# A hybrid SSD, attention and FFN layer on one core: the passage into the FFN and the end of the kernel in written-out orders, and sums, splits and norm weights moved

## The chip, the cores and the metric

The kernel runs on one core of a Trainium2 chip. The metric is the device time of one execution in microseconds, as the median of several runs. Times of single instructions come from one profiled execution of the kernel before; its rows are quoted as the profile prints them, with microseconds from the start of the span. PE is the matrix engine (TensorE), PEld its weight loads, DVE the VectorE, ACT the ScalarE, POOL the GpSimd, SP the engine that issues most DMAs.

## The reference

One layer on a sequence of 1024 tokens of 1024 features, batch 1, all float32:

```python
h = rmsnorm(x, norm_mix_w) * (1 + sc_m) + sh_m
z, xbc, dt_raw, q, k, v = split(h @ w_in)
x = x + g_m * (concat([ssd_mixer(z, xbc, dt_raw), chunk_attention(q, k, v)]) @ w_out)
h = rmsnorm(x, norm_ffn_w) * (1 + sc_f) + sh_f
u = causal_dwconv(h @ w_up, conv_w)          # width 3, FFN 2 x 2816
g, val = split(u)
x = x + g_f * ((silu(g) * val) @ w_down)
out = rmsnorm(x, final_norm_w)
```

The scales, shifts and gates (`sc_m`, `g_f` and so on) come from a product of `silu(c)` with `w_ada`. The change concerns one place in `ssd_mixer` (the cumulative sums of dt), the start of `h @ w_up`, the product with `w_down`, the last residual and the last norm.

## The kernel before

**Products.** Every large product is made in three passes: each operand is split into a high part (ACT copies it into the matrix engine's reduced float32 type) and a low part (DVE subtracts the high part from the operand), and `mm3` (lines 75 to 78) issues high x high, high x low and low x high. So before a product can start, ACT and DVE each have an instruction to do per operand tile, and these are the names that the profile shows: `w` for split weights (hi by ACT, lo by DVE), `tH`/`tL` for split activations.

**The FFN.** `h @ w_up` and the product with `w_down` are done by a Strassen-like scheme with seven products of half the size in each direction, called P1, P2, P3, Q4, Q5, Q6, Q7 (`PRODS`, line 1113). In the up part a *unit* (class `Unit`) is 128 columns of `w_up`; units go in pairs u0 and u1, one for the gate half and one for the value half, in 11 pairs. `sums` forms the weight sums of a unit (rows 4 to 7 of its buffer `b`: `ya` for u0, `xs` for u1), `prep` splits two weight blocks into one *home*, `product` issues the 12 matmuls of a product into a PSUM bank (`uX`, `uY` or `uZ`), and `post` takes the bank off (`cv`, `cg`). Split weights live in a ring of five homes (`HOMES`, `FIRST`, `AGAIN`, lines 1087 to 1095); a new split waits until the product that last used its home is done. The activations that the products need (`t2`, `t3`, `t4`, `b22`) are sums of normalised rows, and for the last rows they are made and split (`h_last`) while the first pair is already on the PE. The raw `t2` lies in the buffer that `cg` takes over.

**Down part.** Seven products (lines 1526 to 1548) with four PSUM banks each (`dn`), the contraction in six steps `m` (11 blocks of 128, so the last step has one block). `split_pair` loads and splits both operands of a step. Results pile up in p1, u2, u3 and q5, four tiles of 128 rows x 512 columns each; `gate` multiplies such a tile by the gate row and adds x (read back from DRAM as `x1d` into two buffers `xts`, on the SP queue); `final` squares a finished row of tiles (ACT), makes the factor (DVE adds two means, POOL raises to -1/2), scales both halves by factor and norm weight (DVE) and stores them (SP).

**What sets the order.** A planner places the instructions of each engine by its own cost model, except between `V.on = A.on = T.on = True` and `False`: there DVE, ACT and PE issue in the order in which the Python code is written (class `InOrder`, from line 45; such instructions carry line 58 in the profile). In the kernel before such a stretch begins at line 800 with the z part and the dt sums (to line 997 on PE, to line 1026 on DVE and ACT), and another is the passage into the FFN, on PE from line 1228, on DVE and ACT from line 1236, to line 1293. From there to the end the planner is free.

Of the kernel before, what the change touches and what calls it, by code (L numbers as in the profile page):

```python
# [16 lines left out]
P = 128  # L17
# [47 lines left out]
def tile_block(ctx: ExitStack, tc: tile.TileContext, x, crep, pk, w_ada, w_first, w_ft, w_z,  # L65
# [1022 lines left out]
    FIRST, AGAIN = (0, 1, 2, 0, 1, 3, 4), (2, 0, 1, 3, 4)  # L1088
# [27 lines left out]
    class Unit:  # L1116
# [29 lines left out]
        def post(self, p, ps):  # L1146
# [11 lines left out]
            elif p == "Q7":  # L1158
                V.tensor_tensor(self.v[:, 512:S], ps, self.v[:, 0:512], ALU.subtract)
                V.tensor_tensor(self.v[:, 512:S], self.v[:, 512:S], self.ps["Z"], ALU.subtract)  # L1160
# [7 lines left out]
            self.done.add(p)  # L1168

# [91 lines left out]
    def h_last(n, src):  # L1261
        for j in range(2):
            h_split(n, src, slice(2 * j, 2 * j + 2))

    h_last("t2", "t2")
    u0.product("P2")
    u1.prep("Q5", "Q6")
# [4 lines left out]
    for u in units:  # L1272
        u.product("Q5")
    h_last("t3", "b12")
    for u in units:
        u.sums((6,))
    for u in units:
        u.prep("Q7", "Q4")
    for u in units:
        u.product("Q6")  # L1280
    h_last("t4", "b21")
    for u in units:
        u.sums((7,))

# [6 lines left out]
    h_last("b22", "b22")  # L1291
    prep_s4(units)
    V.on = A.on = T.on = False
# [77 lines left out]
    for q in range(KH):  # L1371
        if q > 0:
            units = [Unit(q), Unit(KH + q)]
            for u in units:
                u.sums()
        order = ("Q7", "Q4", "P3") if q == 0 else ("P1", "Q6", "Q5", "Q7", "P2", "Q4", "P3")
# [57 lines left out]
    def split_pair(p, m):  # L1434
        ab = [wsplit(t, kn(m)) for t in operands(p, m)]
# [10 lines left out]
    def product(p, ps, ready=(), tail=False, between=None):  # L1446
        last = []
        for m in RM:
# [3 lines left out]
            for k in range(2 * m, 2 * m + kn(m)):  # L1452
                if tail and m >= NM - 2:
                    last.append((ab, k))
                else:
                    step(ps, ab, k, R4)
        return last
# [12 lines left out]
    def final(st, lo, hi):  # L1470
        t = fins[st % 3]
        m = [stat(), stat()]
        for dh, src in enumerate((lo, hi)):
            A.activation(t[:, halves[dh]], src, AF.Square, scale=1.0 / 32.0, accum_out=m[dh])
        r = rstd2(m)
        for dh, src in enumerate((lo, hi)):
            V.scalar_tensor_tensor(t[:, halves[dh]], src, r, fnr[:, halves[dh]], op0=ALU.mult,
                                   op1=ALU.mult)
            nc.sync.dma_start(out[st * P:(st + 1) * P, halves[dh]], t[:, halves[dh]])
# [56 lines left out]
    product("P3", Z)  # L1536
    W = banks("d")
    last = product("P2", W, tail=True)
    for st in R4:
        V.tensor_tensor(u2[st], u2[st], Z[st], ALU.add)  # L1540
    for st in R4:
        gate(u2[st], 4 + st, 0)
        final(4 + st, u2[st], q5[st])
    for st in R4:
        for ab, k in last:
            step(W, ab, k, (st,))
        e = xt_()
        V.tensor_tensor(e, W[st], gf[:, halves[0]], ALU.mult)
        V.tensor_tensor(p1[st], p1[st], e, ALU.add)
        final(st, p1[st], u3[st])  # L1550
# [54 lines left out]
```

## Time and profile before

| what | value |
|---|---|
| median of 3 runs | 1210.14 us (1209.7 to 1210.21) |
| the profiled execution's own time | 1210.66 us |
| its span, first to last instruction | 1208.9 us |
| mean granted clock of the PE | 0.993 |
| PE busy | 1159.7 us (96% of the span) |
| DVE busy | 941.8 us (78%) |
| ACT busy | 594.7 us (49%) |
| POOL busy | 195.3 us (16%) |

A timeline row gives the start, the time taken, the engine, the line, the operation with out<-in, the shapes and the count; at its end in brackets the idle time of the engine just before it and what ended that time. Consecutive matmuls overlap: one of 512 columns takes 0.39 us from start to end, and the next starts 0.227 us after it. A row of the windows view gives, for each engine, the busy time in a stretch and the number of instructions, then the granted clock of the PE and the DMA engines' share.

### The profile page before, as it was taken

The page shows a single profiled execution, that of the slowest core. Times are in us where ns is not written, and L with a number is a line of the kernel's source. Part 1 is how long each engine was busy: PE and PEld are TensorE (multiplying, and loading weights), DVE is VectorE, ACT ScalarE, POOL GpSimd, SP SyncE. Part 2 cuts the span into 40 slices and gives each one's busy share as a digit, 9 for nine tenths or more (in the row PEclk, how much of TensorE's full clock was granted, in tenths as well). Part 3 has the DMA queues.
Part 4 walks back from the last instruction along what each step waited for, and adds up shares of the span by engine and source line. Part 5 has one row for each costly group of instructions (what it writes and reads, how often), then busy time and mean ns, then how long its engine had stood idle before and what let it go on. Part 6 is the DMA issues. An engine that isn't in the chain of part 4 may idle for free.

```text
span 1208.9 us, 15656 instructions
## 1 busy us (share of the span) xinstructions
PE 1159.7 (96%) x5802; PEld 974.6 (81%) x5802; DVE 941.8 (78%) x1413; ACT 594.7 (49%) x1001; POOL 195.3 (16%) x174
## 2 busy tenths in 40 slices
PE   4999999999999999999899999999999999999995
PEld 3887888778879988888788888888888888888884
DVE  7756555598698798657899988898889869666976
ACT  4637464663243777576544433345343445433443
POOL 1108373773120144200000000000000000000001
PEclk9999999999999999999999999999999999999998
DMA  9632121314445301140223333322233278633533
GB/s 355 237 93 88 36 75 35 134 57 152 158 165 175 114 18 54 53 157 36 70 96 113 106 103 123 131 79 87 96 131 114 109 255 303 247 129 115 174 114 139
DMA packets 56683, 151.91 MB, mean 126 GB/s; under 512 B 5664, under 2 KB 5792, under 8 KB 55200
## 3 DMA queue, kind: packets, MB, share of 16 engines
q1 hardware_dynamic: 49552, 126.54, 31.4%
q10 hardware_dynamic: 7056, 24.38, 5.0%
q8 instruction: 45, 0.74, 0.3%
q14 instruction: 30, 0.25, 0.1%
HBM read 117.61 MB, written 29.10 MB: 121 GB/s over the span
## 4 chain that ended last, share of the span: by engine, by line
PE 67%; DVE 7%; ACT 2%; issue 1%; DMA 1%; POOL 0%; SPq 0%; DVEq 0%; POOLq 0%; ACTq 0%
PE dn L76 6%; PE dn L77 6%; PE dn L78 6%; PE wops L705 5%; PE uY L76 5%; PE uY L78 5%; PE uY L77 5%; PE uZ L78 3%; PE uZ L77 3%; PE uZ L76 3%; PE uX L78 3%; PE uX L77 3%; PE uX L76 3%; PE s L76 2%; PE s L77 2%; PE s L78 2%
## 5 line engine op out<-in xcount | busy, mean ns | idle before, releaser
L993 POOL TENSOR_TENSOR st<-st,mhalf 128x1 f32<-128x1 f32 x16 | 12.7, 799 | 692.1 <-DVE st L992 680.5
L76 PE MATMUL dn<-w 128*128 128x512 f32 x308 | 111.9, 389 | 0.0
L77 PE MATMUL dn<-w 128*128 128x512 f32 x308 | 111.9, 389 | 0.0
L78 PE MATMUL dn<-w 128*128 128x512 f32 x308 | 103.3, 389 | 0.0
L76 PE MATMUL uY<-tH,w 128*128 128x512 f32 x256 | 99.7, 389 | 1.8 <-ACT w L58 1.8
L410 POOL TENSOR_SCALAR p<-p,st 128x640 f32<-128x640 f32 (+4 forms) x64 | 98.5, 1554 | 14.4 <-DVE st L409 11.0
L78 PE MATMUL uY<-tH,w 128*128 128x512 f32 x256 | 99.6, 389 | 0.0
L77 PE MATMUL uY<-tL,w 128*128 128x512 f32 x256 | 99.6, 389 | 0.0
L85 ACT ACTIVATE w<-ya 128x1024 fp32r<-128x1024 f32 (+1 forms) x41 | 39.1, 954 | 86.0 <-PE uY L78 82.6
L705 PE MATMUL wops<-hH,yhl 128*128 128x512 f32 x224 | 74.0, 398 | 0.0
L78 PEld LDWEIGHTS dn<-w 128*128 128x128 f32 x308 | 57.8, 188 | 12.1
L76 PEld LDWEIGHTS dn<-w 128*128 128x128 f32 x308 | 57.8, 188 | 12.0
L77 PEld LDWEIGHTS dn<-w 128*128 128x128 f32 x308 | 57.8, 188 | 11.9
L85 ACT ACTIVATE pt<-tp 128x512 fp32r<-128x512 f32 (+2 forms) x72 | 36.6, 523 | 49.5 <-PE tp L436 20.2
L404 DVE CUSTOM_DVE_ANT_0 p<-s,bias 128x640 f32<-128x640 f32 (+4 forms) x64 | 40.7, 650 | 25.5 <-PE s L392 11.0
L86 DVE TENSOR_TENSOR pt<-tp,pt 128x512 fp32r<-128x512 f32 (+2 forms) x72 | 41.9, 596 | 22.9 <-ACT pt L85 14.1
L76 PEld LDWEIGHTS uY<-tH,w 128*128 128x128 f32 x256 | 48.0, 188 | 12.1 <-ACT w L58 2.2
L77 PEld LDWEIGHTS uY<-tL,w 128*128 128x128 f32 x256 | 48.0, 188 | 10.0
L78 PEld LDWEIGHTS uY<-tH,w 128*128 128x128 f32 x256 | 48.1, 188 | 9.9
L85 ACT ACTIVATE w<-xs 128x1024 fp32r<-128x1024 f32 (+1 forms) x41 | 39.0, 952 | 32.1 <-PE uY L78 32.1
L76 PE MATMUL s<-hH,wh 128*128 128x512 f32 x128 | 50.6, 395 | 1.1 <-DVE ct L515 1.1
L86 POOL TENSOR_TENSOR wl<-raws,wh 128x1024 fp32r<-128x1024 f32 x14 | 36.2, 2589 | 93.5 <-ACT wh L85 93.3
(483 smaller groups left out, 3429.5 us busy)
## 6 DMA issues: line engine op xcount, KB each, us to landing
gz<-a ACTq DMA_DIRECT2D x10, 1024.0 KB, 5.3
wos<-in_w_ada_dram SPq DMA_DIRECT2D x18, 512.0 KB, 4.0
ya<-in_w_up_dram SPq DMA_DIRECT2D x11, 768.0 KB, 4.2
xs<-in_w_up_dram SPq DMA_DIRECT2D x11, 768.0 KB, 4.2
adat<-in_w_ada_dram SPq DMA_DIRECT2D x16, 512.0 KB, 6.4
raws<-in_w_ft_dram SPq DMA_DIRECT2D x16, 512.0 KB, 3.6
qk<-in_w_ada_dram SPq DMA_DIRECT2D x14, 512.0 KB, 4.5
gy<-a ACTq DMA_DIRECT2D x10, 512.0 KB, 2.6
```

What stands on the lines that cost most here:

```text
L76: T.matmul(ps, lh, rh, start=start, stop=False, skip_group_check=more)
L77: T.matmul(ps, lh, rl, start=False, stop=False, skip_group_check=more)
L78: T.matmul(ps, ll, rh, start=False, stop=stop, skip_group_check=more)
L85: i = A.activation(hi, src, AF.Copy) if ehi is A else ehi.tensor_copy(hi, src)
L86: return i, elo.tensor_tensor(lo, src, f32(hi), ALU.subtract)
L404: V.tensor_tensor_reduce(out=dst, in0=src, in1=bsl, scale=-1.0, scalar=3e38, op0=ALU.add, op1=ALU.min, accum_out=nm)
L410: G.tensor_scalar(pv_, pv_, rr, None, op0=ALU.mult)
L705: i = op(*a, **k)
L993: G.tensor_tensor(r, ms, mhalf[:, 0:1], ALU.pow)
```

## The change

1. In the z part `dt_sums()` and `pre_x(0)` stand one product (`z_mm(0, 2)`) later.
2. `product` no longer takes its bank off in the same breath: `post` and, for Q7, the subtraction of bank Z (`minus_z`) can be called later.
3. The passage is written in another order: u1's Q5/Q6 weights are split ahead of `h_last("t2")`, Q5 and Q6 of both units follow each other, the halves of the `h_last` splits of t4 and b22 stand between products and their take-off, both Q7 products are in the fixed stretch, and at its end the second pair of units is opened (its loads, its sums 4 and 5, its P1/Q6 splits). The seventh home is the third of the list again and not the fifth, and the cycle after it is (0, 4, 1, 3, 2).
4. A down step with one block puts both operands into one home.
5. During P3 the rows 4 to 7 of u2 are gated before P3's result is there (the result is gated and added by itself in P2), the squares of q5 and u3 are made, and u3 is multiplied by its norm weight.
6. P2 and everything behind it is a fixed stretch. Its last three blocks run row by row as before, each followed by gate product, add and square of that row; the two means are added on POOL; the right half of the rows 0 to 3 is scaled by ACT (a copy with a factor) and stored from ACT's queue, the left half by DVE and SP's queue. The squares write their unused output into a PSUM bank.

The first place is the passage, on ACT, which makes the high parts. `xs` are u1's weights, `rt` the raw t2, `rb_4977` t3, `a` t4, `rb_4978` b22, `uX` the bank of P1 and P2, `cg` the tile that P2 is copied to:

```order
+L58 ACTIVATE w<-xs 128x1024
 L58 ACTIVATE tH_5446<-rt_4976 128x1024 x2
-L58 ACTIVATE cg<-uX 128x512
-L58 ACTIVATE w<-xs 128x1024
-L58 ACTIVATE cg<-uX 128x512
+L58 ACTIVATE cg<-uX 128x512 x2
+L58 ACTIVATE w<-ya 128x1024
 L58 ACTIVATE tH_5446<-rb_4977 128x1024 x2
```

u1's Q5/Q6 weights (`w<-xs`) are ahead of the split of t2 now, and no longer between the two copies of P2. The second place is further on in the passage, on DVE, which makes the low parts; `cv<-uY` takes Q7's bank off:

```order
-L58 TENSOR_TENSOR tL_5449<-a,tH_5448 128x1024 x2
+L58 TENSOR_TENSOR tL_5449<-a,tH_5448 128x1024
+L58 TENSOR_TENSOR cv<-uY,cv 128x512
+L58 TENSOR_TENSOR tL_5449<-a,tH_5448 128x1024
 L58 TENSOR_TENSOR ya<-ya 128x512
 L58 TENSOR_TENSOR xs<-xs 128x512
-L58 TENSOR_TENSOR tL_5449<-rb_4978,tH_5448 128x1024 x2
-L1159 TENSOR_TENSOR cv<-uY,cv 128x512 x2
+L58 TENSOR_TENSOR cv<-uY,cv 128x512
+L58 TENSOR_TENSOR tL_5449<-rb_4978,tH_5448 128x1024
```

Q7 of u0 is taken off between the two halves of t4, not behind all of b22. The third place is the end on DVE, from the first row of P2's result on. Before:

```order
L1548 TENSOR_TENSOR xs<-dn,ya 128x512 x2
L1549 TENSOR_TENSOR cg<-cg,xs 128x512 x2
L1548 TENSOR_TENSOR xs<-dn,ya 128x512 x2
L992 SCALAR_TENSOR_TENSOR st_72<-st_72 128x1
L1549 TENSOR_TENSOR cg<-cg,xs 128x512
L992 SCALAR_TENSOR_TENSOR st_72<-st_72 128x1
L1549 TENSOR_TENSOR cg<-cg,xs 128x512
L1477 SCALAR_TENSOR_TENSOR xs<-cg,st_72,xs 128x512
L1477 SCALAR_TENSOR_TENSOR xs<-dnH_8214,st_72,xs 128x512
```

And now (`xs<-dn,ya` is the gate product, `cg<-cg,xs` the add, `xs<-cg,st_72,xs` the scaling of a left half, `st` the small means and factors):

```order
L58 TENSOR_TENSOR xs<-dn,ya 128x512
L58 TENSOR_TENSOR cg<-cg,xs 128x512
L58 TENSOR_TENSOR xs<-dn,ya 128x512
L58 TENSOR_TENSOR cg<-cg,xs 128x512
L58 SCALAR_TENSOR_TENSOR xs<-cg,st_72,xs 128x512
L58 TENSOR_TENSOR xs<-dn,ya 128x512
L58 TENSOR_TENSOR cg<-cg,xs 128x512
L58 SCALAR_TENSOR_TENSOR xs<-cg,st_72,xs 128x512
L58 TENSOR_TENSOR xs<-dn,ya 128x512
L58 TENSOR_TENSOR cg<-cg,xs 128x512
L58 SCALAR_TENSOR_TENSOR ya<-cg,st_72,xs 128x512
L58 SCALAR_TENSOR_TENSOR xs<-cg,st_72,xs 128x512
```

Before, all four products and adds stood ahead of the first scaling, with eight scalings behind them; now they alternate row by row, and DVE scales four half rows, all of them left halves.

The diff, cut to its core:

```diff
@@ the z part
     r0 = pre_rm(0, 0)
-    dt_sums()
-    x0 = pre_x(0)
     z_evac(0, 1, zp)
     wout_split(0, wt[0])
     zp = z_mm(0, 2, wz)
+    dt_sums()
+    x0 = pre_x(0)
@@ the ring of homes
-    FIRST, AGAIN = (0, 1, 2, 0, 1, 3, 4), (2, 0, 1, 3, 4)
+    FIRST, AGAIN = (0, 1, 2, 0, 1, 3, 2), (0, 4, 1, 3, 2)
@@ class Unit
-        def product(self, p):
+        def product(self, p, post=True, z=True):
...
-            self.post(p, ps)
+            if post:
+                self.post(p)
+            if z and p == "Q7":
+                self.minus_z()
...
             elif p == "Q7":
                 V.tensor_tensor(self.v[:, 512:S], ps, self.v[:, 0:512], ALU.subtract)
-                V.tensor_tensor(self.v[:, 512:S], self.v[:, 512:S], self.ps["Z"], ALU.subtract)
...
+        def minus_z(self):
+            V.tensor_tensor(self.v[:, 512:S], self.v[:, 512:S], self.ps["Z"], ALU.subtract)
@@ the passage
-    h_last("t2", "t2")
-    u0.product("P2")
+    u0.product("P2", post=False)
     u1.prep("Q5", "Q6")
+    h_last("t2", "t2")
+    u0.post("P2")
     u1.product("P2")
...
     for u in units:
         u.product("Q5")
-    h_last("t3", "b12")
     for u in units:
         u.sums((6,))
-    for u in units:
-        u.prep("Q7", "Q4")
-    for u in units:
-        u.product("Q6")
-    h_last("t4", "b21")
+    u0.prep("Q7", "Q4")
+    h_last("t3", "b12")
+    u0.product("Q6")
+    u1.product("Q6")
+    u1.prep("Q7", "Q4")
+    h_last("t4", "b21", (0,))
+    u0.product("Q7", z=False)
+    h_last("t4", "b21", (1,))
     for u in units:
         u.sums((7,))
-    h_last("b22", "b22")
+    u1.product("Q7", z=False)
+    h_last("b22", "b22", (0,))
     prep_s4(units)
+    h_last("b22", "b22", (1,))
+    for u in units:
+        u.minus_z()
+    second = [Unit(1), Unit(KH + 1)]
+    for u in second:
+        u.sums((4, 5))
+    for u in second:
+        u.prep("P1", "Q6")
     V.on = A.on = T.on = False
@@ split_pair
+        if kn(m) == 1:
+            w = ring()
+            ab = [w[:, :, j:j + 1, :] for j in range(2)]
+            for t, src in zip(ab, operands(p, m)):
+                last_split[:] = split(t[:, 0], t[:, 1], src, A, V)
@@ the end
+    mh = {}
+    def p3_rows(m):
+        if m < 4:
+            gate(u2[m], 4 + m, 0)
+            mh[4 + m] = mean(q5[m], fins[m % 3][:, halves[1]])
+        if m > 1:
+            st = m - 2
+            mh[st] = mean(u3[st], fins[m % 3][:, halves[0]])
+            G.tensor_scalar(mh[st], mh[st], EPS, None, op0=ALU.add)
+            V.tensor_tensor(u3[st], u3[st], fnr[:, halves[1]], ALU.mult)
-    product("P3", Z)
+    product("P3", Z, between=p3_rows)
     W = banks("d")
-    last = product("P2", W, tail=True)
-    for st in R4:
-        V.tensor_tensor(u2[st], u2[st], Z[st], ALU.add)
-    for st in R4:
-        gate(u2[st], 4 + st, 0)
-        final(4 + st, u2[st], q5[st])
-    for st in R4:
-        for ab, k in last:
-            step(W, ab, k, (st,))
-        e = xt_()
-        V.tensor_tensor(e, W[st], gf[:, halves[0]], ALU.mult)
-        V.tensor_tensor(p1[st], p1[st], e, ALU.add)
-        final(st, p1[st], u3[st])
+    V.on = A.on = T.on = True
+    ml = {}
+    ab = [split_pair("P2", m) for m in range(2)]
+    for m in RM:
+        rs = {}
+        if m == 0:
+            for st in R4:
+                add_gated(u2[st], Z[st])
+                ml[4 + st] = mean(u2[st], Z[st])
+        elif m < 3:
+            rs = {st: rstd2([ml[4 + st], mh[4 + st]]) for st in (2 * m - 2, 2 * m - 1)}
+        if m + 2 < NM:
+            ab.append(split_pair("P2", m + 2))
+        for st in rs:
+            scale_row(4 + st, u2[st], rs[st], 0)
+            scale_row(4 + st, q5[st], rs[st], 1)
+        if m < NM - 2:
+            for k in range(2 * m, 2 * m + 2):
+                step(W, ab[m], k, R4)
+    def row_out(st):
+        A.activation(fins[st % 3][:, halves[1]], u3[st], AF.Copy, scale=rs[st])
+        store(nc.scalar, st, 1)
+        scale_row(st, p1[st], rs[st], 0)
+    for st in R4:
+        for k in range(2 * NM - 4, KH):
+            step(W, ab[k // 2], k, (st,))
+        add_gated(p1[st], W[st])
+        m, rs[st] = mean(p1[st], W[st]), stat()
+        G.tensor_tensor(m, m, mh[st], ALU.add)
+        G.tensor_tensor(rs[st], m, mhalf[:, 0:1], ALU.pow)
+        if st > 0:
+            row_out(st - 1)
+    row_out(3)
```

More of the change, by code (lines that the diff above doesn't have):

```diff
@@ L1444, in step, with product @@
             mm3(ps[st], b[:, 0, c], b[:, 1, c], a[:, 0, :], a[:, 1, :], k == 0, k == KH - 1)
-    def product(p, ps, ready=(), tail=False, between=None):
-        last = []
+    def product(p, ps, ready=(), between=None):
         for m in RM:
@@ L1452, in product @@
             for k in range(2 * m, 2 * m + kn(m)):
[L1453 to L1457, printed above, removed]
+                step(ps, ab, k, R4)
     def xt_():
@@ new lines, in p3_rows @@
+    def p3_rows(m):
[8 more added lines that the diff above has]
+    product("P3", Z, between=p3_rows)
+    W = banks("d")
+    V.on = A.on = T.on = True
+    V.last = A.last = T.last = None
```

55 lines of the change are left out of this document (31 added, 24 removed).

## The prediction

> **What bounds the kernel now.** I read the page first, for shares and the chain of what ended last.
>
> ```profile
> core 0 of [0], span 1208.9 us
> PE 1159.7 (96%) x5802; PEld 974.6 (81%) x5802; DVE 941.8 (78%) x1413; ACT 594.7 (49%) x1001; POOL 195.3 (16%) x174
> PE 67%; DVE 7%; ACT 2%; issue 1%; DMA 1%; POOL 0%; SPq 0%; DVEq 0%; POOLq 0%; ACTq 0%
> ```
>
> PE is busy for all but 49.2 us. The change leaves the number of matmuls alone, so it can only win where PE waits, where its clock is down, or behind its last matmul. I looked for these places in the windows view (busy time of PE, PEld, DVE, ACT, POOL, then PE's clock, DMA share, GB/s):
>
> ```profile
> 575.00:580.00 5.00, 4.03 (x12) 2.94 (x13) 4.37 (x5) 2.92 (x5) 0.00 (x0) 0.78 0.01 2
> 580.00:585.00 5.00, 5.00 (x21) 4.06 (x20) 3.47 (x4) 5.00 (x6) 0.00 (x0) 0.88 0.31 105
> 600.00:640.00 40.00, 40.00 (x178) 33.13 (x177) 40.00 (x48) 19.60 (x21) 0.00 (x0) 1.00 0.32 112
> 640.00:700.00 60.00, 60.00 (x267) 49.67 (x266) 56.37 (x68) 26.84 (x31) 0.00 (x0) 1.00 0.29 99
> 1150.00:1190.00 40.00, 40.00 (x178) 33.12 (x177) 31.14 (x43) 18.03 (x29) 5.26 (x4) 1.00 0.37 130
> ```
>
> From 600 us on PE never stops; DVE stands at 40.00 of 40 there, then at 56.37 of 60, and near the end at 31.14 of 40. Ahead of 560 us the change touches one place only. So three are left: the dt sums, the passage at 573 to 594 us with a clock of 0.78 and 0.88, and the tail.
>
> **The dt sums (part 1).** PE in the timeline of the z part:
>
> ```profile
> 401.30 0.28 PE L58 MATMUL s<-wzh,hL 128*128 128x260 f32 x1
> 402.39 0.43 PE L58 MATMUL tp<-sm_e,tle 128*128 128x64 f32 x2 [0.80 <-DVE sm_e L58]
> ```
>
> Matmuls of 260 columns follow each other by 0.12 us, so the step of 1.09 holds 0.97 of waiting for DVE's dt chain. Moved behind `z_mm(0, 2)`, the sums get that product's 24 matmuls in front of them, 24 × 0.12 = 2.9 us, three times what was missing. Without that cover the wait would be the old one. I take −1.0 (0.8 to 1.0).
>
> **The passage (parts 2 and 3).** PE, DVE, ACT in the timeline:
>
> ```profile
> 573.51 0.39 PE L58 MATMUL uZ<-t1h,w 128*128 128x512 f32 x1
> 575.45 0.50 PE L58 MATMUL uZ<-t1h,w 128*128 128x512 f32 x1 [1.54 <-ACT w L58]
> 575.78 0.40 PE L58 MATMUL uZ<-t1l,w 128*128 128x512 f32 x1
> 576.71 0.74 PE L58 MATMUL uZ<-t1h,w 128*128 128x512 f32 x2 [0.53 <-DVE w L58]
> ...
> 578.57 1.05 PE L58 MATMUL uZ<-t1h,w 128*128 128x512 f32 x2
> ...
> 591.39 0.39 PE L78 MATMUL uY<-tH,w 128*128 128x512 f32 x1
> 593.56 0.47 PE L76 MATMUL uY<-tH,w 128*128 128x512 f32 x1 [1.78 <-ACT w L58]
> ```
>
> ```profile
> 571.40 2.35 DVE L58 TENSOR_TENSOR tL<-rt,tH 128x1024 fp32r<-128x1024 f32 x2
> ...
> 590.46 2.35 DVE L58 TENSOR_TENSOR tL<-rb,tH 128x1024 fp32r<-128x1024 f32 x2
> 592.73 1.28 DVE L1159 TENSOR_TENSOR cv<-uY,cv 128x512 f32<-128x512 f32 x2
> ```
>
> ```profile
> 573.85 0.60 ACT L58 ACTIVATE cg<-uX 128x512 f32<-128x512 f32 x1 [2.19 <-DVE tL L58]
> 574.34 1.05 ACT L58 ACTIVATE w<-xs 128x1024 fp32r<-128x1024 f32 x1
> ...
> 592.84 0.63 ACT L58 ACTIVATE w<-ya 128x512 fp32r<-128x512 f32 x1 [7.19 <-DVE tL L58]
> ```
>
> Against a step of 0.227 us the three stalls lose 575.45 − 573.51 − 0.23 = 1.71, 576.71 − 575.78 − 0.23 = 0.70 and 593.56 − 591.39 − 0.23 = 1.94, together 4.35 us. The first two have one cause: `cg` takes the buffer of the raw t2, so ACT's copy waits for DVE's `tL` of t2 (571.40 to 573.75), and u1's Q5 weights stand behind that copy on ACT. The change splits these weights first. The third is ACT's last weights and Q7's take-off (592.73), both behind DVE's b22 low parts (590.46 to 592.81); in the new order Q7 is taken off between the halves of t4. So all three go, −4.35.
>
> What is late next? I walked DVE's new order with the steps above (a 1024-wide subtraction 1.13 behind its like, from 2.35 x2; a 512-wide one 0.6, from 1.28 x2) and one more row, the convolution's step:
>
> ```profile
> 614.56 2.47 DVE L1175 SCALAR_TENSOR_TENSOR a<-cg,pkt,a 128x1023 f32<-128x1023 f32 x2
> ```
>
> DVE runs without a gap from u1's Q6 take-off to the low part of the second pair's Q5 weights: 17 steps of 0.6, 5 of 1.13, one convolution of 1.2 and that low part, 1.22: 18.3 us. PE has six products of 12 matmuls (Q7, Q4 and P3 of both units) and six early matmuls of the second pair in that time, 78 × 0.227 = 17.7, and the take-off starts about 0.2 behind the start of PE's next matmul. That leaves a wait of 0.8. Then PE does 10 matmuls, 2.3 us, and needs u1's bank Z, which DVE frees 0.6 + 1.2 + 0.6 + 0.7 = 3.1 later: another 0.8. I take +1.5 in all. Both are differences of long sums: 1 us better on DVE removes the first, 2 us worse brings a stall as large as the old ones. Bounds 0 and +4.35. **Passage: −2.85.**
>
> The second pair's loads and sums, now in the fixed stretch, have this row:
>
> ```profile
> ya<-in_w_up_dram SPq DMA_DIRECT2D x11, 768.0 KB, 4.2
> ```
>
> Their buffers come free at the fourth sums (589.25 in before, earlier now), the first use is some 6 us later, so 4.2 us fit with about 2 to spare; if a load were late, the P1 high parts would be, up to 2 us.
>
> **The clock.** Behind the first two stalls the matmul pair at 578.57 takes 1.05 where 0.39 + 0.23 = 0.62 is usual: steps of some 0.43 for 0.23, and the windows show 0.78 and 0.88. The missing clock is 5 × 0.22 + 5 × 0.12 = 1.7 us; from eight matmuls at 0.2 more it is 1.6. The third stall, 1.94 us alone, brought none:
>
> ```profile
> 590.00:595.00 5.00, 3.22 (x14) 2.36 (x13) 4.52 (x6) 1.15 (x2) 0.00 (x0) 1.00 0.82 264
> ```
>
> So 2.4 us of idleness within 3.2 us triggers it, 1.9 does not, and the new waits are 0.8 and 0.8 within 3.9. I take −1.6. [...]
>
> **Part 4 and 5, the end of P3.** One home for a one-block step takes a wait off PE's path or changes nothing. Gating P3's result apart costs DVE four more products and four more adds, less four adds, and u3's norm product moves four in front: about four net 512-wide steps, 2.8 us. Near the end DVE idles for 40 − 31.14 = 8.9 us; ACT, which takes the early squares, is at 18.03 of 40. Zero, and 2.8 us without that cover.
>
> **Part 6, the start of P2**, now in written order. The `x1d` loads of the gates have two buffers, and their times to landing are
>
> ```profile
> L1467 SPq DMA_DIRECT2D xs<-x1d x16: 319/333/431, 1069.0 to 1173.7; - x16
> ...
> DMA to landing us min/median/max: 2.6/4.3/5.7
> ```
>
> Call P2's first matmul S. The fourth gate's load can be issued when the second gate's add is done, by my walk S − 3.0; landing after 2.7 gives the add at S + 0.4, one low part S + 1.5, four dependent products and adds of 1.32 each S + 6.9, the last square and two high parts S + 9.7, and the second low part of step m = 2 at S + 11.1. PE wants it after two steps of 24 matmuls and two more, S + 11.3. So 0.2 to spare with a quick load, and with the median of 4.3 (its chain runs through two gates) 2.0 of waiting. The load stands behind no weight load at that point, so I sit near the quick end: **+0.3** (0 to 2.0).
>
> **Part 6, the tail.** The rows before:
>
> ```profile
> 1194.55 0.39 PE L78 MATMUL dn<-w 128*128 128x512 f32 x1
> ...
> 1193.85 1.29 DVE L1548 TENSOR_TENSOR xs<-dn,ya 128x512 f32<-128x512 f32 x2 [4.71 <-PE dn L78]
> 1195.05 1.28 DVE L1549 TENSOR_TENSOR cg<-cg,xs 128x512 f32<-128x512 f32 x2
> ...
> 1204.40 0.75 DVE L1477 SCALAR_TENSOR_TENSOR xs<-cg,st,xs 128x512 f32<-128x512 f32 x1 [0.66 <-POOL st L993]
> 1205.07 0.75 DVE L1477 SCALAR_TENSOR_TENSOR xs<-dnH,st,xs 128x512 f32<-128x512 f32 x1
> ...
> 1202.39 0.63 ACT L1474 ACTIVATE xs<-dnH 128x512 f32<-128x512 f32 x1
> 1202.93 0.19 ACT L1474 ACTIVATION_READ_ACCUMULATOR xs<-dnH 128x1 f32 x1
> ...
> 1203.82 0.55 POOL L993 TENSOR_TENSOR st<-st,mhalf 128x1 f32<-128x1 f32 x1 [1.60 <-DVE st L992]
> ```
>
> From E = 1194.94 to 1208.9 are 13.96 us; from the last scaling's end (1205.82) to the end, the store and its landing, 3.1. The last row alone now: product 0.69, add 0.69, square 0.63 + 0.19, add of means on POOL 0.55 and power 0.55 (both from the row of the power), scaling 0.75, end 3.1, with some 0.2 of hand-overs: E + 7.4. It is not alone. In DVE's written order row 2's scaling stands between row 3's add and row 3's scaling, and POOL is caught by DVE:
>
> ```profile
> 1182.87 2.06 POOL L993 TENSOR_TENSOR st<-st,mhalf 128x1 f32<-128x1 f32 x1 [3.54 <-DVE st L992]
> ...
> 1182.71 1.22 DVE L86 TENSOR_TENSOR w<-dnL,w 128x1024 fp32r<-128x1024 f32 x1
> 1183.85 0.69 DVE L86 TENSOR_TENSOR w<-dna,w 128x512 fp32r<-128x512 f32 x1
> ```
>
> The same tiny power took 2.06 us here and ended 0.4 behind DVE's second subtraction; beside an idle DVE it takes 0.55. Now two POOL steps per row run while DVE multiplies and adds the next row, 1.3 us of it. If a caught step costs until the running DVE pair is over, row 3, whose POOL steps meet only row 2's scaling, is later by about 1.0: E + 8.4. Two stores at once instead of one may add up to 0.7: E + 9.2. I take 8.4, −5.55 (−6.7 to −4.8). [...]
>
> **The sum.** −1.0 − 2.85 − 1.6 + 0.3 − 5.55 = −10.7. From the profiled execution's 1210.66: 1199.96. That execution is 0.5 above the median of the runs, 1210.14; so 1199.4 for the median.
>
> **Rivals.**
> (a) *The half clock stays.* It came at the same place behind 2.4 us of waiting; the new waits are 1.6 in 3.9 us. It would give 1201.0.
> (b) *The start of P2 waits for `x1d`.* For it: the median landing of 4.3 and 0.2 to spare. Against: little traffic there. 2.0 instead of 0.3: 1201.1; with (a), 1202.7.
> (c) *DVE's backlog eats the passage.* The passage ends sooner, DVE's work does not shrink, and 600 to 640 us shows it at 40.00 of 40. If the second and third pair must wait for it, PE gives back the passage's 2.85 and the clock's 1.6: 1203.9. Against it: PE had no wait there though DVE was full, and DVE takes the second pair's sums in order.
> (d) *Slower.* The new ring cycle (0, 4, 1, 3, 2) makes one split in each pair wait for a home that is still read. At DVE's 56.37 of 60 there is 0.3 us of slack per product; a split that starts one product (2.72) late cannot be caught up. Five pairs at 2.72 are 13.6: about 1213. It decides from the first pair that meets a home one product later than before. Against it: the cycle has as many homes as before.
>
> **How the numbers follow.** Chances: forecast 0.63, (a) 0.15, (b) 0.10, (c) 0.07, (d) 0.05. The likeliest case by itself spans 1197 to 1201: 1.5 less in the passage and 1.1 in the tail on one side (not both in full), 0.7 in the tail and 1 in the passage on the other. The range takes in (a) and (b) and ends short of (c) and (d): 1197.0 to 1203.4. A run of this kernel cannot tell less than some 0.2%, 2.4 us, from no change. All cases but (d) are 6 us or more below before, so faster 0.93, slower 0.05, and 0.02 for a mixture of (c) and (d) that ends near zero.
>
> **What would show it.** Right: the step before the `tp` matmul of the dt sums at 0.12; no wait above 1 us between u0's Q5 and the second pair's Q5; a clock of 1.00 in that stretch; 7.4 to 9.2 us from the last matmul's end to the span's end, with POOL rows over 1 us in it. Wrong: a wait for DVE `w` of more than 2 us near the second pair's Q5, a clock below 1.00 behind the passage, PE idle in P2 at its third step with DVE's `x1d` add late before it, or any recurring wait per pair after 600 us.

## The result and the profile after

| | before | after |
|---|---|---|
| median of 5 runs | 1210.14 us (1209.37 to 1210.46) | 1199.29 us (1198.77 to 1199.39) |
| profiled execution, span | 1210.66 us, 1208.9 us | 1198.77 us, 1197.1 us |
| end of PE's last matmul | 1194.94 | 1189.44 |
| from there to the end of the span | 13.96 us | 7.66 us |

The ratio is 0.9911, with a 95% interval from 0.9896 to 0.9925; 1199.4 us was forecast. Between the two profiled executions lie 11.9 us, between the medians 10.85: the profiled run of before is 0.5 us above its median, that of after 0.5 below. The terms are compared in the profiled pair, where the spans differ by 11.8 us:

| term | forecast | from the traces |
|---|---|---|
| dt sums | −1.0 | −1.1 |
| three stalls of the passage | −4.35 | −4.35 |
| new waits in their place | +1.5 | +1.26 |
| slow clock | −1.6 | −1.6 |
| start of P2 | +0.3 | 0.0 |
| tail | −5.55 | −6.30 |

The sum of the right column is −12.1, 0.3 us more than the spans differ by. By the starts of PE's matmuls the passage brings 4.5 us (the k-th matmul starts 0.98 us later in before at 560 us, 5.50 from 610 us on) where its terms add up to 4.7: the steps next to the waits are longer too, by 0.4 us in all before and 0.6 after, which the terms leave out. The other 0.1 us is drift ahead of 400 us. For the profiled execution 1199.96 us was forecast and 1198.77 came, so a difference of 0.1 us between forecast and median is closer than the terms are.

First the page of the changed kernel, then its windows view:

```profile
span 1197.1 us, 15659 instructions
PE 1157.9 (97%) x5802; PEld 973.6 (81%) x5802; DVE 943.6 (79%) x1413; ACT 595.8 (50%) x1005; POOL 199.9 (17%) x182
```

```profile
575.00:580.00 5.00, 5.00 (x24) 4.14 (x23) 4.11 (x5) 3.33 (x5) 0.00 (x0) 1.00 0.31 105
...
595.00:600.00 5.00, 4.60 (x20) 3.23 (x19) 5.00 (x8) 5.00 (x6) 0.00 (x0) 1.00 0.00 0
600.00:640.00 40.00, 39.48 (x174) 32.30 (x173) 39.77 (x47) 17.94 (x21) 0.00 (x0) 1.00 0.32 112
```

The passage runs at a clock of 1.00 and PE is full there, up to two waits around 600 us. PE's timeline has them, and the dt sums:

```profile
404.29 0.28 PE L58 MATMUL zps<-wzh,hL 128*128 128x260 f32 x1
404.40 0.33 PE L58 MATMUL tp<-sm_e,tle 128*128 128x64 f32 x2
...
599.44 0.50 PE L78 MATMUL uZ<-t1h,w 128*128 128x512 f32 x1 [0.40 <-DVE w L86]
...
602.53 0.47 PE L76 MATMUL uZ<-t1h,w 128*128 128x512 f32 x1 [0.52 <-DVE cg L1170]
```

The dt matmul follows the z product after 0.11 us. The two waits are the ones that the walk of DVE's order named: the low part of the second pair's Q5 weights, then u1's bank Z. With the matmul step of 0.23 taken off they cost 0.57 and 0.69 us (0.8 and 0.8 forecast). DVE's stretch in front of the first one, from the start of u1's Q6 take-off (581.09) to the end of that low part (599.39), took 18.30 us, as its walk said.

The tail of the changed kernel, PE, DVE, ACT and POOL in the timeline:

```profile
1169.78 19.66 PE L58 MATMUL dn<-w 128*128 128x512 f32 x86
...
1183.36 0.69 DVE L58 TENSOR_TENSOR xs<-dn,ya 128x512 f32<-128x512 f32 x1 [1.30 <-PE dn L58]
...
1189.48 0.69 DVE L58 TENSOR_TENSOR xs<-dn,ya 128x512 f32<-128x512 f32 x1
1190.20 0.69 DVE L58 TENSOR_TENSOR cg<-cg,xs 128x512 f32<-128x512 f32 x1
1190.81 0.74 DVE L58 SCALAR_TENSOR_TENSOR ya<-cg,st,xs 128x512 f32<-128x512 f32 x1
1192.58 0.75 DVE L58 SCALAR_TENSOR_TENSOR xs<-cg,st,xs 128x512 f32<-128x512 f32 x1 [1.02 <-POOL st L1609]
...
1192.73 0.72 ACT L58 ACTIVATE xs<-dnH,st 128x512 f32<-128x512 f32 x1 [0.47 <-POOL st L1609]
...
1191.73 0.19 POOL L1608 TENSOR_TENSOR st<-st 128x1 f32<-128x1 f32 x1 [1.22 <-ACT dn L58]
1192.00 0.55 POOL L1609 TENSOR_TENSOR st<-st,mhalf 128x1 f32<-128x1 f32 x1
```

Row 0's product starts 6.08 us ahead of PE's end (1183.36 against 1189.44), where before it started 1.09 ahead (1193.85 against 1194.94). Behind row 3's matmuls there is one chain: product, add, square, two POOL steps of 0.19 and 0.55, the scaling of the two halves on DVE and ACT at once, and from there to the end of the span 3.8 us behind DVE's scaling (1193.33) or 3.6 behind ACT's, the later one (1193.45).

### The profile page after: what moved, and what is told of

It is laid out like the page before. It is cut to its first block, busy times and chain, and to the rows that moved or that the text cites. A ratio compares the mean times of both kernels' runs of the same rounds, so it can differ in the third digit from the quotient of the medians.

```text
span 1197.1 us, 15659 instructions
## 1 busy us (share of the span) xinstructions
PE 1157.9 (97%) x5802; PEld 973.6 (81%) x5802; DVE 943.6 (79%) x1413; ACT 595.8 (50%) x1005; POOL 199.9 (17%) x182
## 4 chain that ended last, share of the span: by engine, by line
PE 68%; DVE 7%; ACT 1%; DMA 1%; issue 1%; SPq 0%; ACTq 0%; DVEq 0%
PE wops L705 5%; PE dn L77 5%; PE dn L76 5%; PE dn L78 5%; PE uY L78 5%; PE uY L76 5%; PE uY L77 5%; PE uX L78 3%; PE uX L76 3%; PE uX L77 3%; PE uZ L76 3%; PE uZ L78 3%; PE uZ L77 3%; PE dn L58 2%; PE s L76 2%; PE s L77 2%
## 5 line engine op out<-in xcount | busy, mean ns | idle before, releaser
L1565 POOL TENSOR_SCALAR st<-st 128x1 f32<-128x1 f32 x4 | 3.9, 983 | 587.9 <-ACT ya L1490 584.6
L77 PE MATMUL dn<-w 128*128 128x512 f32 x264 | 97.8, 389 | 0.0
L76 PE MATMUL dn<-w 128*128 128x512 f32 x264 | 97.2, 389 | 0.0
L77 PE MATMUL uY<-tL,w 128*128 128x512 f32 x248 | 96.5, 389 | 0.0
L76 PE MATMUL uY<-tH,w 128*128 128x512 f32 x248 | 96.5, 389 | 0.0
L78 PE MATMUL uY<-tH,w 128*128 128x512 f32 x248 | 96.5, 389 | 0.0
L78 PE MATMUL dn<-w 128*128 128x512 f32 x264 | 92.0, 389 | 0.0
L76 PEld LDWEIGHTS dn<-w 128*128 128x128 f32 x264 | 49.6, 188 | 10.3
L78 PEld LDWEIGHTS dn<-w 128*128 128x128 f32 x264 | 49.6, 188 | 10.2
L77 PEld LDWEIGHTS dn<-w 128*128 128x128 f32 x264 | 49.6, 188 | 10.2
L78 PEld LDWEIGHTS uY<-tH,w 128*128 128x128 f32 x248 | 46.6, 188 | 9.6
L76 PEld LDWEIGHTS uY<-tH,w 128*128 128x128 f32 x248 | 46.6, 188 | 9.6
```

What stands on the lines that cost most here:

```text
L76: T.matmul(ps, lh, rh, start=start, stop=False, skip_group_check=more)
L77: T.matmul(ps, lh, rl, start=False, stop=False, skip_group_check=more)
L78: T.matmul(ps, ll, rh, start=False, stop=stop, skip_group_check=more)
L1565: G.tensor_scalar(mh[st], mh[st], EPS, None, op0=ALU.add)
```

## The experiments

A time of one of these kernels is uncertain by a good 1 us, so small terms are read from the traces: the start of PE's k-th matmul is compared between two executions, ahead of the edit and behind it. Ahead of 560 us these executions differ by up to 1.9 us without any cause in the code; that is taken off below. A part of it is the clock: in most traces it is at half near 238 us for 3.41 us, in the three with the largest shift (the first piece back, and the two old ends with a further edit) for 6.83 us.

**The dt sums back.**

```diff
+    dt_sums()
+    x0 = pre_x(0)
     z_evac(0, 1, zp)
     wout_split(0, wt[0])
     zp = z_mm(0, 2, wz)
-    dt_sums()
-    x0 = pre_x(0)
```

> The changed kernel with the dt sums and x at their old place, ahead of the take-off of the second z block. Theory (each term of the sum stands where it was said): PE's step ahead of the dt matmul is 1.0 to 1.1 us again, PE's last matmul ends 1.0 us later than in the changed kernel, the tail stays, so 1200.3 us. Rival (the time up to the passage does not matter, since DVE sets the pace there): the step comes back, and is given back before 610 us, so 1199.3.

```profile
402.47 0.28 PE L58 MATMUL s<-wzh,hL 128*128 128x260 f32 x1
403.56 0.43 PE L58 MATMUL tp<-sm_e,tle 128*128 128x64 f32 x2 [0.81 <-DVE sm_e L58]
```

The step of 1.09 is back, and PE stays 1.1 us late to its last matmul: nothing is given back. 1200.86 us. The theory holds; the time by itself is 0.6 above the expected 1200.3, less than it can tell.

**The first piece of the passage back.**

```diff
-    u0.product("P2", post=False)
-    u1.prep("Q5", "Q6")
     h_last("t2", "t2")
-    u0.post("P2")
+    u0.product("P2")
+    u1.prep("Q5", "Q6")
     u1.product("P2")
```

> The changed kernel with the first piece of the passage in the old order: the split of t2 ahead of P2 and of u1's Q5 and Q6 weights. Theory: two stalls of 1.7 and 0.7 to 0.8 us return, the slow clock behind them returns for 3.4 us (1.6 us), and the two waits near the second pair's Q5 (0.57 and 0.69) stay, since DVE's chain starts from the Q6 take-off: PE ends 4.0 us later, 1203.3 us. [...]

```profile
574.17 0.39 PE L58 MATMUL uZ<-t1h,w 128*128 128x512 f32 x1
576.11 0.50 PE L58 MATMUL uZ<-t1h,w 128*128 128x512 f32 x1 [1.55 <-ACT w L58]
576.45 0.40 PE L58 MATMUL uZ<-t1l,w 128*128 128x512 f32 x1
577.37 0.73 PE L58 MATMUL uZ<-t1h,w 128*128 128x512 f32 x2 [0.53 <-DVE w L58]
...
578.18 0.62 PE L58 MATMUL uZ<-t1h,w 128*128 128x512 f32 x2
```

The stalls are those of before to a few hundredths, 1.71 and 0.69, but behind them a pair of matmuls takes 0.62, not 1.05: the clock stays at 1.00. PE is 2.7 us late from here to the end, and the median is 1202.11 (+2.8), 1.2 below the theory's 1203.3. So the order of these splits is worth 2.4 to 2.7 us by itself, and the theory fails at the clock: the slow clock of before did not follow from the sum of its stalls.

**Q7 taken off behind all of b22, as before.**

```diff
-    u0.product("Q7", z=False)
+    u0.product("Q7", post=False, z=False)
     h_last("t4", "b21", (1,))
     for u in units:
         u.sums((7,))
-    u1.product("Q7", z=False)
-    h_last("b22", "b22", (0,))
+    u1.product("Q7", post=False, z=False)
+    h_last("b22", "b22")
     prep_s4(units)
-    h_last("b22", "b22", (1,))
+    for u in units:
+        u.post("Q7")
```

> The changed kernel with Q7 of both units taken off behind all of b22, as before. Theory (DVE sets the pace from the Q6 take-off to the second pair's Q5): PE waits 4.0 us for bank Y ahead of Q4 by a walk of DVE's order, the two later waits (1.26) vanish, because DVE has caught up, and with 4 us of idleness in one piece the clock is down for 3.4 us (1.6 us): 1199.3 + 4.0 - 1.3 + 1.6 = 1203.6; without the slow clock 1202.0. Rival (the stalls are independent of each other): the old 1.94 us returns and the later waits stay, 1201.2 us.

```profile
587.59 0.39 PE L58 MATMUL uY<-tH,w 128*128 128x512 f32 x1
592.10 0.77 PE L76 MATMUL uY<-tH,w 128*128 128x512 f32 x1 [4.12 <-DVE cv L58]
```

PE waits 592.10 − 587.59 − 0.23 = 4.3 us for bank Y, and the clock is halved behind it, for 6.8 us and not the 3.4 expected. The two waits near 600 us are gone, as the theory has it: DVE has caught up while PE stood still. PE is 5.3 us late at the end, the median 1204.18 (+4.9; 1203.6 forecast). The stalls are not independent: from 581 us, where it last waits for PE, to 603 us DVE runs without a gap and sets the pace.

**Stalls of chosen length, for the clock.** In pairs 2 to 9, with PE in written order (`n_late` lists the widths of the copies for the pair; its table is left out here):

```diff
+                    if n_late and p == "P1" and u is units[0]:
+                        one = stat()
+                        V.tensor_scalar(one, u.v[:, 0:1], 0.0, 1.0, op0=ALU.mult, op1=ALU.add)
+                        for cols in n_late:
+                            A.activation(u.w["Q6"][:, 0, 0:cols], f32(u.w["Q6"][:, 0, 0:cols]), AF.Copy, scale=one)
```

> The changed kernel with one made stall of PE in each of eight later pairs: between the take-off of the first unit's P1 and its Q6 weights' high part stands a chain of repeated ACT copies (of the value onto itself), so many that PE waits, by a walk of the order, 1.4, 1.4, 2.3, 2.6, 3.4, 2.3, 1.4 and 3.4 us. One stall in one piece each. Theory of the prediction (idleness of 2.4 us within some 3.2 halves the clock, 1.9 does not): slow clock behind the stalls of 2.6 and 3.4, none behind 1.4, in doubt at 2.3. [...] Time: 1199.3 plus 18.2 of stalls plus 1.5 to 1.7 or more for each slow stretch, 1218 to 1230 us.

The stalls came out at 1.15, 1.46, 1.89, 2.21, 2.64, 2.05, 1.46 and 2.81 us, and the clock fell twice, behind 2.21 and 2.81, but not behind 2.64. They are shorter than planned, so a made stall of 3.4 us was not seen. 1218.72 us in its single run. The clock changes on a grid of 3.413 us: in before at 236.42, 239.83, 577.75, 581.17 and 1198.98 us, whole multiples of it apart, and here the two falls behind made stalls, at 772.70 and 936.54 us, are 48 such steps apart. The windows view of this kernel, cut on its grid (the number behind PE's busy time is that of its matmuls; of 512 columns, at 0.227 us each, about 15 fit at full rate):

```profile
769.29:772.70 3.41, 1.36 (x7) 0.81 (x6) 2.15 (x4) 2.52 (x4) 0.00 (x0) 1.00 0.49 199
772.70:776.11 3.41, 3.41 (x10) 2.66 (x9) 0.00 (x0) 0.00 (x0) 0.00 (x0) 0.50 0.64 262
...
810.25:813.66 3.41, 1.76 (x8) 1.13 (x6) 3.22 (x5) 3.18 (x6) 0.00 (x0) 1.00 0.18 73
813.66:817.07 3.41, 2.58 (x11) 2.16 (x12) 0.00 (x0) 0.75 (x2) 0.00 (x0) 1.00 0.95 388
...
933.13:936.54 3.41, 1.07 (x5) 0.89 (x6) 1.19 (x2) 2.23 (x4) 0.00 (x0) 1.00 0.80 327
936.54:939.95 3.41, 3.41 (x10) 2.64 (x9) 0.00 (x0) 0.00 (x0) 0.00 (x0) 0.50 0.33 135
```

The stall of 2.64 us lies across a border, 8 matmuls on the one side and 11 on the other, and leaves no mark; that of 2.21 lies in one window, 7 matmuls, and halves the clock for the next window. The kernel before, on its own grid:

```profile
574.34:577.75 3.41, 1.78 (x7) 1.17 (x8) 2.12 (x2) 3.41 (x5) 0.00 (x0) 1.00 0.01 2
577.75:581.17 3.42, 3.42 (x10) 2.65 (x9) 2.90 (x5) 1.34 (x3) 0.00 (x0) 0.50 0.08 17
...
591.41:594.82 3.41, 1.63 (x8) 1.08 (x7) 2.93 (x5) 1.15 (x2) 0.00 (x0) 1.00 0.90 330
```

and the run with the first piece of the passage back:

```profile
572.62:576.03 3.41, 1.94 (x9) 1.28 (x7) 1.80 (x2) 1.51 (x3) 0.00 (x0) 1.00 0.01 2
576.03:579.45 3.42, 2.81 (x11) 2.04 (x12) 2.84 (x4) 2.02 (x4) 0.00 (x0) 1.00 0.10 23
```

The same two stalls fell into one window of before (7 matmuls) and into two windows here (9 and 11). In the passage and in the made stalls, windows with 3, 5 or 7 long matmuls were followed by the half clock, those with 8 or more were not; busy time alone does not sort them (1.78 before a slow window, 1.63 before a full one). Nor does the count draw a sharp line: at the end of the last version below, a window with 7 is followed by one at the full clock, in which no matmul runs any more:

```profile
1186.79:1190.21 3.42, 1.56 (x7) 0.94 (x6) 3.35 (x6) 2.02 (x5) 1.29 (x3) 1.00 0.67 249
1190.21:1193.62 3.41, 0.00 (x0) 0.00 (x0) 1.01 (x2) 1.69 (x4) 0.74 (x2) 1.00 0.72 270
```

The view counts a matmul that only touches the window, too; the seventh of before starts on its border (577.75). So what exactly is weighed stays open. That the place of a stall on the grid decides is shown, and the rule of the prediction falls. The half clock came twice behind a window with 7 matmuls, in which PE was busy for 1.36 and for 1.78 of its 3.41 us.

**Slack at the start of P2.**

```diff
+            for _ in range(3):
+                V.tensor_tensor(u2[0], u2[0], u2[0], ALU.max)
             for st in R4:
                 add_gated(u2[st], Z[st])
```

> The changed kernel with three more DVE steps of 0.6 us (the maximum of a tile with itself) ahead of the four gated rows at the start of P2. Theory (the splits of P2's third step are ready only 0.2 to 0.4 us before PE wants them): PE waits 1.4 to 1.9 us at the third step in all, 1200.9 us. Rival (DVE's idle time of 1.7 us ahead of these splits is slack, so at most 0.1 us shows): 1199.4 us.

```profile
1171.36 0.81 PE L58 MATMUL dn<-w 128*128 128x512 f32 x2 [0.57 <-ACT w L58]
1172.80 1.43 PE L58 MATMUL dn<-w 128*128 128x512 f32 x5 [0.64 <-DVE w L58]
```

1.8 us more on DVE made PE 1.9 us late, in two waits at the third step, and the median 1201.18 (+1.9). There is no cover left: in the changed kernel the last low part of this step ends at 1167.94 + 2.36 = 1170.30, and PE wants it at 1170.24 + 0.23:

```profile
1167.94 2.36 DVE L58 TENSOR_TENSOR w<-dnH,w 128x1024 fp32r<-128x1024 f32 x2 [1.74 <-ACT w L58]
```

DVE's idle 1.74 us in front of it is a wait for ACT, whose squares wait for DVE's adds, so it is no slack.

**The old end.** Everything from P3's banks on as in the kernel before (its block from `Z = banks("e")` on, with `final` and the `tail` of `product`).

> The changed kernel with everything from P3's banks to the end as in the kernel before: no early squares and gates during P3, P2 placed by the planner, four products and four adds ahead of all scalings, squares written into the output tiles, all scalings on DVE. Theory: PE's last matmul ends where it does in the changed kernel (189.4 behind 1000 us, within 0.3), and the tail is as long as before, 13.5 to 14.0 us for 7.7, so 1205.5 us. Rival (part of the 6.3 us comes from P2's own new order or from DVE's lead): the last matmul moves by more than 0.5 us.

**The old end with the squares' output in PSUM.**

```diff
-            A.activation(t[:, halves[dh]], src, AF.Square, scale=1.0 / 32.0, accum_out=m[dh])
+            A.activation(junk, src, AF.Square, scale=1.0 / 32.0, accum_out=m[dh])
```

> As the run with the old end, but the squares write their unused output into a PSUM bank. In the kernel before, the last row's square waited 2.7 us until the store of row 0 out of the same output tile was through. Theory A (the buffer is a cause by itself): the tail is 2 to 2.7 us shorter than with the old end, 1203 us. Theory B (DVE's order, with two squares, two factors and eight scalings behind all adds, is what counts): the tail is the same within 0.7 us, 1205 us.

**The old end with PE held to the written order.**

```diff
+    T.on, T.last = True, None
     for st in R4:
         for ab, k in last:
             step(W, ab, k, (st,))
```

> As the run with the old end, but PE alone is held to the written order in the last three blocks, row by row; DVE and ACT stay with the planner. Theory (in the old end the planner had shuffled the rows on PE, so that all four rows ended within the last microseconds, and that is a part of the gain by itself): the first row's product starts 6 us ahead of PE's end, and the tail is 10.0 to 10.5 us, between 12.6 with the old end and 7.7 in the changed kernel: 1202.2 us. Rival (the eight scalings and DVE's order are all of it): the tail stays above 12 us.

| kernel | tail in the trace | median |
|---|---|---|
| before | 13.96 us | 1210.14 us |
| old end | 12.64 us | 1204.66 us |
| old end, squares into PSUM | 12.56 us | 1204.19 us |
| old end, PE row by row | 10.50 us | 1202.30 us |
| changed kernel | 7.66 us | 1199.29 us |

The old end's tail is 12.6 us, not the 13.5 to 14.0 expected. The starts of PE's matmuls do not shift against the changed kernel between P3 and the end in any of the three: P2's new order is worth nothing on PE itself. DVE in the old end, then with the squares in PSUM, then with PE row by row, the first product each:

```profile
1188.20 1.29 DVE L1584 TENSOR_TENSOR xs<-dn,ya 128x512 f32<-128x512 f32 x2 [4.87 <-PE dn L78]
...
1196.03 0.63 ACT L1510 ACTIVATE xs<-cg 128x512 f32<-128x512 f32 x1 [2.71 <-DVE st L992]
```

```profile
1188.89 1.29 DVE L1584 TENSOR_TENSOR xs<-dn,ya 128x512 f32<-128x512 f32 x2 [4.93 <-PE dn L78]
...
1193.89 0.58 ACT L1510 ACTIVATE dn<-cg 128x512 f32<-128x512 f32 x1
```

```profile
1185.36 0.69 DVE L1585 TENSOR_TENSOR xs<-dn,ya 128x512 f32<-128x512 f32 x1 [1.25 <-PE dn L58]
```

The buffer is not it: with the squares in PSUM row 3's square starts at 1193.89, with no wait of 2.7 us before it, and the tail is the same. (The planner also put the squares of all four right halves into the tail there; ACT is through with them at 1195.82, and DVE adds the last means at 1197.17, so they are not what held the end.) The order on PE is: in row order the first product starts 6.1 us ahead of PE's end (1191.44) and the tail is 2.1 us shorter, as expected. In the old ends that the planner made, the first products start only 1 to 2.5 us ahead of it, because the planner had shuffled the rows' matmuls. The 1.3 us between before and the old end go with another such shuffle (1.09 and 2.45 us ahead); that was not tried by itself. What is left from 10.5 to 7.66 is the order on DVE and ACT, the early squares and norm weights, and the right halves on ACT. The last of these was undone by itself, in the next run, and is worth 0.8 us; the other 2.0 were not taken apart.

**The right halves back on DVE.**

```diff
-        A.activation(fins[st % 3][:, halves[1]], u3[st], AF.Copy, scale=rs[st])
-        store(nc.scalar, st, 1)
         scale_row(st, p1[st], rs[st], 0)
+        V.tensor_scalar(fins[st % 3][:, halves[1]], u3[st], rs[st], None, op0=ALU.mult)
+        store(nc.sync, st, 1)
```

> The changed kernel with the right halves of the last four rows scaled by DVE behind the left halves (one factor per row, the norm weight is in u3 already) and stored from SP's queue, not scaled by ACT and stored from ACT's queue. Theory (DVE then has more to do per row, product, add and two scalings of 0.6 to 0.7 each, than PE's 2.04 us per row, so it falls behind from row to row): the tail is 9.0 to 9.5 us for 7.7, 1200.8 us. Rival (only the last row's second scaling is added, the others fit into DVE's idle time of 0.6 us per row): the tail is 8.1 to 8.4 us, 1199.9 us.

```profile
1190.79 0.68 DVE L58 TENSOR_TENSOR xs<-dn,ya 128x512 f32<-128x512 f32 x1
...
1192.12 0.74 DVE L58 SCALAR_TENSOR_TENSOR ya<-cg,st,xs 128x512 f32<-128x512 f32 x1
1192.79 0.48 DVE L58 TENSOR_SCALAR ya<-dnH,st 128x512 f32<-128x512 f32 x1
```

The tail is 8.46 us, 0.8 longer, between the theory (9.0 to 9.5) and the rival (up to 8.4); 1200.02 us. The mechanism is the theory's: row 3's product starts 0.74 us behind PE's end (1190.05), for 0.04 in the changed kernel, since DVE needs 2.39 us per row and PE 2.04. The size was off, because a scaling without the norm weight takes a step of 0.40 and not 0.66. That the norm weight was multiplied into u3 ahead saves DVE this 0.26 us per right half.

**What holds POOL.** Three DVE additions beside row 3's POOL steps, with both operands in SBUF (shown), or one of them in PSUM (`W[0]` for `q5[0]`):

```diff
+    for _ in range(3):
+        V.tensor_tensor(u2[0], q5[0], q5[1], ALU.add)
     row_out(3)
```

> The changed kernel with three more DVE additions of two SBUF tiles (0.6 us each, 1.8 us, into a tile no longer needed) between row 2's and row 3's scaling, while POOL does the two small steps of row 3. Theory of the prediction (a POOL step that starts while DVE runs two-input instructions back to back ends only 0.4 us behind the last of them): the two POOL steps, 0.19 and 0.55 us in the changed kernel, take 1.5 to 2.3 us in all, and the last scaling starts 1.3 to 1.8 us later than in the changed kernel. Rival (POOL is not held back in the tail, DVE alone is in the way): 0.19 and 0.55 as before, the last scaling 0.7 us later.

> The same with one of the two operands of the three additions in a PSUM bank. Theory (what holds POOL back is two inputs from SBUF, which explains why the gate products from a PSUM bank left it alone in the changed kernel): POOL's steps take 0.19 and 0.55 us, the last scaling starts 0.7 us later than in the changed kernel. Rival (any busy DVE holds POOL back): as in the run with two SBUF tiles.

Both in SBUF:

```profile
1192.78 0.48 POOL L1608 TENSOR_TENSOR st<-st 128x1 f32<-128x1 f32 x1 [1.22 <-ACT dn L58]
1193.34 1.01 POOL L1609 TENSOR_TENSOR st<-st,mhalf 128x1 f32<-128x1 f32 x1
...
1192.53 2.13 DVE L58 TENSOR_TENSOR cv<-ya 128x512 f32<-128x512 f32 x3
1194.58 0.74 DVE L58 SCALAR_TENSOR_TENSOR xs<-cg,st,xs 128x512 f32<-128x512 f32 x1
...
1194.38 0.72 ACT L58 ACTIVATE xs<-dnH,st 128x512 f32<-128x512 f32 x1 [1.06 <-POOL st L1609]
```

One in PSUM:

```profile
1192.21 0.19 POOL L1608 TENSOR_TENSOR st<-st 128x1 f32<-128x1 f32 x1 [1.22 <-ACT dn L58]
1192.48 0.55 POOL L1609 TENSOR_TENSOR st<-st,mhalf 128x1 f32<-128x1 f32 x1
...
1191.96 2.14 DVE L58 TENSOR_TENSOR cv<-dn,ya 128x512 f32<-128x512 f32 x3
1194.01 0.74 DVE L58 SCALAR_TENSOR_TENSOR xs<-cg,st,xs 128x512 f32<-128x512 f32 x1
```

Beside two SBUF operands the steps take 0.48 and 1.01 us, beside one in PSUM 0.19 and 0.55. So the theory of what holds POOL stands in both runs. What it costs DVE's half was overrated: POOL's last step ended (1194.35) before the last addition did (1194.66), and DVE's scaling starts 0.94 us later than in the changed kernel, measured from row 3's add, in both runs (1.3 to 1.8 and 0.7 expected), because DVE itself is busy until then. On ACT, which waits for POOL alone, the hold does show: measured in the same way the right half starts 0.6 us later with both operands in SBUF and no later with one in PSUM. The tails are 8.4 and 7.9 us (1200.60 and 1199.53 us, single runs).

**A version that beats both.** The first pair's convolution of the value half is held back on DVE behind the take-off of P3:

```diff
         if q < KH - 1:
+            if q == 0:
+                with tc.issue_after(units[1].p3):
+                    for u in units:
+                        u.conv(1, u.v)
             for u in units:
                 u.finish()
...
-                self.conv(1, self.v)
+                if self.i % KH:
+                    self.conv(1, self.v)
             elif p == "P3":
-                V.tensor_tensor(self.g[:, 512:S], self.g[:, 512:S], ps, ALU.add)
+                self.p3 = V.tensor_tensor(self.g[:, 512:S], self.g[:, 512:S], ps, ALU.add).ins
```

> The changed kernel with the first pair's convolution of the value half held back on DVE until the first pair's P3 is taken off in both units: two convolution steps of 1.2 us stand behind the low parts and bank takes-offs that PE waits for, not ahead of them. Theory (the two waits left are DVE's order alone): both waits go, 1.26 us, no other takes their place: 1198.0 us. Rival (DVE is full from 600 to 640 us, so work put off comes back as a wait in the second or third pair): PE's last matmul where it was, 1199.3 us.

The waits view of its PE has no entry from 560 us on; in the changed kernel it has the two waits shown above. 1197.98 us, a ratio to before of 0.9900 (0.9885 to 0.9914). PE is 1.7 us earlier from 603 us to its end, so nothing comes back in the later pairs. That is 0.4 more than the two waits of 1.26, because the longer steps next to them go too (the first behind each is 0.33 and 0.31 us, for 0.227). Against the changed kernel the medians differ by 1.3 us, which the runs alone could not tell from nothing; the trace can.

## Why the prediction was right, point by point

- **The dt sums**: right in size, cause and permanence; the run that undid them gave 1.1 us back.
- **The passage**: the three stalls went as said, and both waits that took their place stood where the walk of DVE's order put them, with the releasers that it named; 1.26 us for 1.5. That all these stalls have their cause in DVE's and ACT's order is what the two runs with pieces put back show, and the run with the convolution held back shows the same of the waits left.
- **The clock**: the size was right for this pair of executions, −1.6, the reason was wrong. The step "2.4 us of idleness within 3.2 us triggers it, 1.9 does not" fell: the same stalls left the clock alone when they fell into two windows of the 3.413 us grid. Of the changed kernel it can be said that no window in the passage comes near 7 matmuls: its two waits leave 12 at least, and 11 in the other runs that have them. Whether each execution of the kernel before had the slow stretch cannot be told from its one trace. So this term belongs to the execution, and part of the agreement with 1199.4 is luck.
- **Start of P2**: 0.0 for +0.3; the 0.2 us of slack in the working were 0.17 in the trace (its S + 6.9 adds up to 6.8, and its 2.0 us for a median landing is not worked out: 1.6 us later, once or through two gates, is 1.4 or 3.0 with the slack off), and rival (b) did not come, with loads that landed after 2.6 to 5.8 us, 3.7 in the median.
- **Parts 4 and 5**: nothing, as said: PE's distance to before stays at 5.50 us from 610 us to its end, and the runs with the old end, which undo part 5, show no shift of PE. Part 4 was not undone by itself.
- **The tail**: mis-sized, −5.55 for −6.30, with three errors in E + 8.4 against 7.66, which in part cancel. POOL's hold was put at 1.0 and was 0, and the sign that was named for it, POOL rows over 1 us in the tail, did not come. The step that failed is "row 3, whose POOL steps meet only row 2's scaling": that scaling (1190.81 to 1191.55) was through before POOL's steps began (1191.73), so they met an idle DVE. In rows 0 to 2 POOL's steps begin beside gate products, which read PSUM, and took 0.19 and 0.55 too. The add of the means was put at 0.55 and took 0.19. The stores were put at 3.1 and took 3.8 behind DVE's scaling, because two run at once: the slower of the two landed 2.6 us after its issue, for 2.0 to 2.1 in before (with one operand in PSUM above, where ACT's store is issued 0.8 us ahead of SP's, it is 3.1 again); that 0.7 stood in the working as a bound and was not taken. On the other side, the old tail was taken as it stood without its cause: the text ahead of the prediction says "row by row as before", as the code is written, but the planner had shuffled these rows on PE, and that alone is 2.1 us in the old end of the experiments. The bound of −6.7 is also 0.1 beyond what E + 7.4 gives, −6.6.
- **Rivals**: (a) did not come: the half clock behind a wait is real, as the run of Q7 shows for 4.3 us, but the two waits of 0.57 and 0.69 us leave 12 matmuls or more in each window, and no window of the passage or the made stalls with 8 or more was followed by it. (c) and (d) fell: PE's matmuls start 5.5 us ahead of before at 610 us, and still do at the last one. The slack of 0.3 us per product in (d) is too high: 3.63 us idle in 60, 22 products, is 0.16.

## What to carry to other kernels

Where an engine's order is left to a planner, read the trace for the order that came out, above all in the last microseconds: that the rows of the result were done in turn on PE alone was worth 2.1 us here. Where one engine sets the pace, a removed stall comes back in part as the next item on its list (4.35 us removed, 1.26 back), and walking its order instruction by instruction gives place and size of what comes next. And a clock that fell behind a stall is not a property of the order: the same two stalls, of 1.7 and 0.7 us, were followed by the half clock in one trace and not in the other, so ask how the stall lies on the clock's grid, of 3.413 us here, before its cost is put into a sum.

## What the runs showed of the hardware

- PE's clock changed on a grid of 3.413 us. Of the windows with few matmuls of 512 columns (about 15 fit), those with 5 or fewer and two of three with 7 were followed by a window at half rate, those with 8 or more were not; by half of 3.413 us a slow window costs an estimated 1.7 us, and the one of before cost 1.6. A stall of 2.64 us across a border cost nothing more, one of 2.21 within a window did.
- Small POOL steps were stretched from 0.19 and 0.55 to 0.48 and 1.01 us beside DVE additions of two SBUF tiles, and not at all when one operand came from PSUM.
- Ahead of 560 us, executions of nearly equal programs differed by up to 1.9 us. Most of it arose up to 260 us. In three of them 1.3 us of it arose where the half clock near 238 us lasted two windows for one; the cause of the rest was not tried.
